# A two-block decoder on one core: streamed operands at one address residue, and the delta rule's triangular solve moved from GpSimd to VectorE

## The chip, the cores and the metric

The kernel runs on 1 core of one Trainium2 chip. The metric is the device time of one execution in microseconds, lower is better: the median of three runs before is 1069.82 us (1067.52 to 1071.11).

## What is computed

Two decoder blocks over 256 tokens of width 1024, all in float32. The first block mixes tokens by a gated delta rule (8 heads) and by forgetting attention (8 heads); the second has two SwiGLU layers around an attention mixer. The part that the change rewrites is the delta rule, a chunk at a time:

```python
a_mat = jnp.where(tri_strict, beta[..., None] * kk * decay, 0.0)
rhs = jnp.concatenate([v * beta[..., None], k * (beta * jnp.exp(G))[..., None]], axis=-1)
sol = lax.linalg.triangular_solve(a_full, rhs, left_side=True, lower=True, unit_diagonal=True)
...
def step(s, inp):
    v_new = value_c - jnp.einsum('bhcd,bhde->bhce', kcum_c, s)
    o = (jnp.einsum('bhcd,bhde->bhce', qdec_c, s) + jnp.einsum('bhcs,bhse->bhce', attn_c, v_new))
    s = s * dec_c[..., None, None] + jnp.einsum('bhcd,bhce->bhde', kdec_c, v_new)
    return s, o
```

Around it stand the weight products: `w_in` (q, k, v, z, gates of both mixers), `w_proj_gdn`, `w_proj_fox`, `w_out`, an MLP of width 4096 (relu squared), then in block 2 `gate`, `up` and `down` of width 2816 twice, and a mixer's `w_in` and `w_out`.

## The kernel before

**Weight products.** Every float32 product is made of three TensorE matmuls (hi times hi, hi times lo, lo times hi). A weight tile of 128x128 is the stationary operand, an activation tile of 128 x 256 tokens streams past it. L249 to L251 are the three matmuls of the common form, L280 to L282 a form with 512 columns, L321 to L323 the products of part of the inner dimension. SP loads raw weights, 1 MB at a time, into three buffers; ScalarE casts the high part (`wh`, L213), VectorE subtracts it for the low part (`wl`, L214), into five buffers each. The activations that stream lie in the tiles `Ah`, `Al`, `Bh`, `Bl`, `ah`, `al`, `oa2`, `ob2` (h for high, l for low), each put by `operand` with an offset of its own:

```python
    off = {"Ah": 40, "Al": 0, "Bh": 8, "Bl": 0}
```

**Order.** One generator yields the weight products in their order (the main line), others (the sides) yield the small work of norms, heads and groups with a PE time and a wait; `Lines` steps a side when its wait is over. A scheduler then sorts the instructions of each engine by a timeline of its own. What comes out is a fixed list for each engine, which runs in that order: an instruction that waits holds up all that stand behind it.

**The delta rule.** `gdn_group` handles two heads in two chunks of 128 tokens (four 128x128 matrices); there are four groups. Each makes the decay matrix by matmuls of `sel` with the rows of gate sums (L683, L684), the products K K and K Q (L696), the scaled matrix `bm` (L699), and inverts it: the diagonal blocks of 16 are cut out by DMA (`img`, then `blk`), solved by 15 steps of two GpSimd instructions (`stmp` L724, `sol` L728), put back by DMA (`inv`, then `tt`), transposed (L749), and doubled to 32, 64 and 128 by matmuls (L763, L771, L774, L780, L785). Then come the applications to V and the state (L793 to L820), the norm of the output by an inverse root on GpSimd (L139 to L147), and a transpose back (L840). Groups 0 and 1 run beside the `w_in` products, groups 2 and 3 beside `w_in`, `w_proj_fox` and the first half of `w_proj_gdn`. Forgetting attention adds its gate sums by `sel` matmuls as well (L925, L927).

After the groups the first half of the rows of `w_proj_gdn` (heads of groups 0 and 1) is multiplied, each pair of tiles being taken up by VectorE (`zt`, L1051) and GpSimd (L1054); the second half needs the output of groups 2 and 3; `w_out` follows.

Of the kernel before, what the change touches and what calls it, by code (L numbers as in the profile page):

```python
# [8 lines left out]
F32 = mybir.dt.float32  # L9
# [220 lines left out]
MM = 0.109  # L230
# [101 lines left out]
def xpair(g, slot):  # L332

    off = {"Ah": 40, "Al": 0, "Bh": 8, "Bl": 0}
    return tuple(operand(g.xp, KT, off[slot + p], slot + p, nm(g, slot + p)) for p in "hl")


def gemm_add(g, src, nk, x, scale, nxt):

    for m in range(0, KT, 2):  # L340
        if m + 2 < KT:
# [17 lines left out]
class Norm:  # L359
# [69 lines left out]
    def scales(self):  # L429

        g, nc = self.g, self.g.nc
        self.column()
        yield 1.0, 7.5
# [71 lines left out]
def gates_small(g, pool, ps, u):  # L505

    nc = g.nc
    zr = pool.tile([24, T], F32, tag="zr", name="zr")
# [67 lines left out]
    g.beta, g.ngc, g.eg, g.ed, g.rows = beta, ngc, eg, ed, rows  # L576
# [44 lines left out]
def image_views(flat):  # L621

    image = flat.rearrange("(i r) x -> i (r x)", i=4)[:, 0 : P * P].rearrange("i (s c) -> s i c", c=P)
    diag = flat[:, 0:2048].rearrange("b (j c) -> b j c", c=P)[:, :, 0:16]
    return image, diag


def gdn_group(g, grp, have, zg):

    nc = g.nc  # L630
    h0 = grp * 2
    par = grp % 2
# [18 lines left out]
    beta, ngc, eg = cols(g.beta), cols(g.ngc), cols(g.eg)  # L651
    ed = g.ed[:, h0 : h0 + 2]
    x0, x1, at, uu, tt, xp, xq, xk = (buf(n) for n in ("x0", "x1", "at", "uu", "tt", "xp", "xq", "xk"))


    ss = small([P, 8], "ss")
    pk, pq = bank(), bank()
    for a, b in ((0, pk), (1, pq)):
        for i, (h, c) in enumerate(inst):
            nc.tensor.transpose(b[:, i], kq[:, a, h, c * P : (c + 1) * P], g.ident)  # L660

    kdn, ken = xk[:, 0:2], xk[:, 2:4]
# [11 lines left out]
    nc.vector.tensor_scalar_add(sk, sk, 4 * EPS)  # L674

    nc.vector.reciprocal(bk2, sk)
    nc.vector.tensor_tensor(out=bk2, in0=bk2, in1=beta, op=ALU.mult)
    yield 0.0, 0.0

    dec = x0  # L680
    pd = raw_bank().rearrange("p (h n) -> p h n", h=2)
    for h in range(2):
        nc.tensor.matmul(pd[:, h], lhsT=g.sel[h0 + h], rhs=g.rows, start=True, stop=False)  # L683
        nc.tensor.matmul(pd[:, h], lhsT=g.identr, rhs=g.mgdnr, start=False, stop=True)  # L684
    for i, (h, c) in enumerate(inst):
        nc.scalar.activation(
            out=dec[:, i], in_=pd[:, h, c * P : (c + 1) * P], func=AF.Exp, bias=ngc[:, i : i + 1]
        )
    yield 0.45, 0.0

    bm = x1
# [13 lines left out]

    flat = g.dr.tile([32, 2064], F32, tag="img", name=nm(g, "img"), bufs=4)
    image, diag = image_views(flat)
    inv_image, inv_diag = image_views(g.inv[par])
    blk = g.gs.tile([32, 16, 16], F32, tag="blk", name=nm(g, "blk"))
    sol = g.gs.tile([32, 16, 16], F32, tag="sol", name=nm(g, "sol"))  # L710
    tmp = g.gs.tile([32, 64], F32, tag="stmp", name=nm(g, "stmp"))
    nc.sync.dma_start(out=image, in_=bm)
    yield 0.0, 0.0
    nc.sync.dma_start(out=blk, in_=diag)
# [3 lines left out]
    gp.tensor_tensor(out=nkv, in0=nkv, in1=r, op=ALU.mult)  # L718
    gp.tensor_scalar(out=base, in0=ss[:, 4:8], scalar1=P * EPS, scalar2=4 * P * EPS * EPS, op0=ALU.mult, op1=ALU.add)
    gp.tensor_copy(sol, g.con["eye16"][0:32].rearrange("p (i k) -> p i k", k=16))  # L720
    for jj in range(15):
        n, m = 15 - jj, jj + 1
        t = tmp[:, : n * m].rearrange("p (i k) -> p i k", k=m)
        gp.tensor_tensor(  # L724
            out=t, in0=blk[:, jj, m:].unsqueeze(2).to_broadcast([32, n, m]),
            in1=sol[:, jj, 0:m].unsqueeze(1).to_broadcast([32, n, m]), op=ALU.mult,
        )
        gp.tensor_tensor(out=sol[:, m:, 0:m], in0=sol[:, m:, 0:m], in1=t, op=ALU.subtract)  # L728
        if jj % 3 == 2:
            yield 0.0, 0.0  # L730
# [11 lines left out]
    nc.sync.dma_start(out=inv_diag, in_=sol)  # L742
    yield 0.0, 0.0
    for i in range(2):
        nc.sync.dma_start(out=tt[:, 2 * i : 2 * i + 2], in_=inv_image[:, 2 * i : 2 * i + 2])
    yield 0.0, 0.0
    pt = bank()
    for i in range(4):
        nc.tensor.transpose(pt[:, i], tt[:, i], g.ident)  # L749
    nc.scalar.copy(uu, pt)  # L750

    for lev, b in enumerate((16, 32)):
        def half(a, side):
            v = a.rearrange("p i (n t b) -> p i n t b", t=2, b=b)
            return v[:, :, :, side]

        p2 = (xp, xq)[lev % 2]
        nc.gpsimd.memset(half(p2, 1), 0.0)
        mask = g.con[f"m{b}"].rearrange("p (n b) -> p n b", b=b)
        nb = 64 // b  # L760
        pp = raw_bank()[:, :256].rearrange("p (i n b) -> p i n b", i=4, b=b)
        for i in range(4):
            nc.tensor.matmul(pp[:, i], lhsT=bm[:, i], rhs=half(tt, 0)[:, i], start=True, stop=True)  # L763
        nc.vector.tensor_tensor(
            out=half(p2, 0), in0=pp, in1=mask.unsqueeze(1).to_broadcast([P, 4, nb, b]), op=ALU.mult
        )
        yield 0.45, 0.0
        pu = raw_bank()[:, :256].rearrange("p (i n b) -> p i n b", i=4, b=b)
        pe = raw_bank()[:, :256].rearrange("p (i n b) -> p i n b", i=4, b=b)
        for i in range(4):  # L770
            nc.tensor.matmul(pe[:, i], lhsT=uu[:, i], rhs=half(p2, 0)[:, i], start=True, stop=True)  # L771
        nc.vector.tensor_tensor(out=half(tt, 0), in0=half(tt, 0), in1=pe, op=ALU.subtract)
        for i in range(4):
            nc.tensor.matmul(pu[:, i], lhsT=p2[:, i], rhs=half(uu, 1)[:, i], start=True, stop=True)  # L774
        nc.vector.tensor_tensor(out=half(uu, 1), in0=half(uu, 1), in1=pu, op=ALU.subtract)
        yield 0.9, 0.0
    lo, up = slice(0, 64), slice(64, P)
    pp = raw_bank()[:, :256].rearrange("p (i n) -> p i n", i=4)
    for i in range(4):
        nc.tensor.matmul(pp[up, i], lhsT=bm[lo, i, up], rhs=tt[lo, i, lo], start=True, stop=True)  # L780
    nc.vector.tensor_copy(xp[up, :, lo], pp[up])
    yield 0.45, 0.0
    pu = raw_bank()[:, :256].rearrange("p (i n) -> p i n", i=4)
    for i in range(4):
        nc.tensor.matmul(pu[lo, i], lhsT=xp[up, i, lo], rhs=uu[up, i, up], start=True, stop=True)  # L785
    nc.vector.tensor_tensor(out=uu[lo, :, up], in0=uu[lo, :, up], in1=pu[lo], op=ALU.subtract)
    yield 0.45, 0.0

    vnew = x0
# [761 lines left out]
```

## Time and profile before

| what | value |
|---|---|
| median of three runs | 1069.82 us |
| the profiled execution | 1070.23 us |
| its span, first to last instruction | 1068.4 us |
| PE busy | 1041.8 us, 98% |
| VectorE (DVE) busy | 658.7 us, 62% |
| ScalarE (ACT) busy | 566.5 us, 53% |
| GpSimd (POOL) busy | 271.4 us, 25% |
| mean granted clock of PE | 0.993 |

Engine time is time in instructions of that engine; a matmul's busy time overlaps its neighbour's, so that the pace of PE is better read from how many matmuls a stretch of the span holds than from the length of one.

### The profile page before, as it was taken

Reading aid. Unit: us, or ns where it says so; the run is one execution under the profiler, and the core shown is the slowest. Engines: PE = TensorE matmul, PEld = TensorE weight load, DVE = VectorE, ACT = ScalarE, POOL = GpSimd, SP = SyncE. Lnnn points to the kernel's source line nnn. Section 1 sums busy time; section 2 is a strip of 40 time slices with the busy share of each in tenths; the row PEclk is TensorE's granted clock in tenths of the full one; section 3 lists DMA queues with packets and bytes.
Section 4 is the critical chain, followed back from the end, with each engine's and each line's share of the span. In section 5 each row is a group of like instructions: output and inputs, shape, how many; then the busy total and the mean of one; then the engine's idle time right before and its main releaser. Section 6 shows DMA issues by size and latency. Waiting matters only on the chain.

```text
span 1068.4 us, 20471 instructions
## 1 busy us (share of the span) xinstructions
PE 1041.8 (98%) x8326; PEld 1004.9 (94%) x8326; DVE 658.7 (62%) x943; ACT 566.5 (53%) x1040; POOL 271.4 (25%) x561
## 2 busy tenths in 40 slices
PE   8999999999899899999999999999999999999997
PEld 7778899899899899999999999999989899999996
DVE  6565874757345687764555665586676576656453
ACT  6775674467345356664444444445575755444442
POOL 3635336326504240000012211141204531111000
PEclk9999999999899999999999999999999999999999
DMA  8553335334424355555454555466644445544551
GB/s 307 204 190 119 125 140 174 121 118 149 134 99 142 119 208 184 198 197 182 174 198 160 195 186 175 143 235 208 225 136 166 145 158 198 175 182 160 163 184 47
DMA packets 36271, 179.61 MB, mean 168 GB/s; under 512 B 7632, under 2 KB 11856, under 8 KB 18384
## 3 DMA queue, kind: packets, MB, share of 16 engines
q1 hardware_dynamic: 35296, 175.15, 47.2%
q0 software_dynamic: 448, 2.62, 0.7%
q8 instruction: 65, 1.06, 0.4%
q10 hardware_dynamic: 432, 0.53, 0.1%
q14 instruction: 30, 0.25, 0.1%
HBM read 175.54 MB, written 2.75 MB: 167 GB/s over the span
## 4 chain that ended last, share of the span: by engine, by line
PE 82%; POOL 9%; DMA 3%; DVE 2%; issue 2%; ACT 1%; SPq 0%; DVEq 0%; POOLq 0%; ACTq 0%
PE g L251 21%; PE g L250 21%; PE g L249 21%; PE g L282 2%; PE g L280 2%; PE g L281 2%; POOL sol L728 2%; POOL stmp L724 1%; DVE wl L214 1%; POOL rsq L144 1%; POOL rsq L145 1%; POOL rsq L146 1%; PE g L321 1%; PE g L322 1%; PE g L323 1%
## 5 line engine op out<-in xcount | busy, mean ns | idle before, releaser
L214 DVE TENSOR_TENSOR wl<-raw,wh 128x1024 fp32r<-128x1024 f32 (+2 forms) x347 | 418.6, 1211 | 263.3 <-ACT wh L213 261.3
L213 ACT CAST wh<-raw 128x1024 fp32r<-128x1024 f32 (+2 forms) x347 | 344.6, 999 | 377.1 <-PE g L250 340.1
L250 PE MATMUL g<-Bl,wh 128*128 128x256 f32 x832 | 234.0, 282 | 0.8 <-DVE Bl L169 0.8
L251 PE MATMUL g<-Bh,wl 128*128 128x256 f32 x832 | 234.0, 282 | 0.6 <-DVE wl L214 0.6
L249 PE MATMUL g<-Bh,wh 128*128 128x256 f32 x832 | 232.4, 281 | 0.0
L251 PE MATMUL g<-Ah,wl 128*128 128x256 f32 x776 | 218.2, 282 | 0.0
L250 PE MATMUL g<-Al,wh 128*128 128x256 f32 x776 | 218.2, 282 | 0.0
L249 PE MATMUL g<-Ah,wh 128*128 128x256 f32 x776 | 217.8, 282 | 0.0
L251 PE MATMUL g<-ah,wl 128*128 128x256 f32 x608 | 171.3, 282 | 1.5 <-DVE wl L214 1.5
L249 PE MATMUL g<-ah,wh 128*128 128x256 f32 x608 | 171.4, 282 | 0.0
L250 PE MATMUL g<-al,wh 128*128 128x256 f32 x608 | 171.4, 282 | 0.0
L250 PEld LDWEIGHTS g<-Bl,wh 128*128 128x128 f32 x832 | 156.7, 188 | 1.2 <-DVE Bl L169 1.2
L251 PEld LDWEIGHTS g<-Bh,wl 128*128 128x128 f32 x832 | 156.7, 188 | 0.9 <-DVE wl L214 0.8
L249 PEld LDWEIGHTS g<-Bh,wh 128*128 128x128 f32 x832 | 156.1, 188 | 0.0
L249 PEld LDWEIGHTS g<-Ah,wh 128*128 128x128 f32 x776 | 146.9, 190 | 0.5 <-ACT fv L163 0.2
L250 PEld LDWEIGHTS g<-Al,wh 128*128 128x128 f32 x776 | 146.7, 189 | 0.6
L251 PEld LDWEIGHTS g<-Ah,wl 128*128 128x128 f32 x776 | 146.8, 189 | 0.3
L251 PEld LDWEIGHTS g<-ah,wl 128*128 128x128 f32 x608 | 115.3, 190 | 1.7 <-DVE wl L214 1.7
L250 PEld LDWEIGHTS g<-al,wh 128*128 128x128 f32 x608 | 115.4, 190 | 0.0
L249 PEld LDWEIGHTS g<-ah,wh 128*128 128x128 f32 x608 | 115.2, 190 | 0.0
L1112 POOL TENSOR_TENSOR s<-s,row 128x512 f32<-128x512 f32 x22 | 36.9, 1679 | 184.2 <-ACT s L1111 184.2
L395 POOL TENSOR_TENSOR acc<-acc,sq 128x512 f32<-128x512 f32 x10 | 13.9, 1393 | 237.5 <-ACT sq L390 237.5
(332 smaller groups left out, 1444.8 us busy)
## 6 DMA issues: line engine op xcount, KB each, us to landing
raw<-in_w_in_dram SPq DMA_DIRECT2D x44, 1024.0 KB, 4.8
raw<-in_ffn_gu_dram SPq DMA_DIRECT2D x44, 1024.0 KB, 4.8
raw<-in_ffn_dn_dram SPq DMA_DIRECT2D x32, 704.0 KB, 4.1
raw<-in_w_up_dram SPq DMA_DIRECT2D x16, 1024.0 KB, 4.7
raw<-in_w_down_dram SPq DMA_DIRECT2D x16, 1024.0 KB, 4.7
raw<-in_w_out_dram SPq DMA_DIRECT2D x8, 1024.0 KB, 4.7
raw<-in_w_proj_fox_dram SPq DMA_DIRECT2D x4, 1024.0 KB, 4.9
raw<-in_w_proj_gdn_dram SPq DMA_DIRECT2D x4, 1024.0 KB, 4.8
```

Of the source, the lines that this page charges most:

```text
L144: e.tensor_tensor(out=t, in0=y, in1=y, op=ALU.mult)
L213: nc.scalar.copy(hi[:, r], raw[:, r])
L214: nc.vector.tensor_tensor(out=lo[:, r], in0=raw[:, r], in1=hi.bitcast(F32)[:, r], op=ALU.subtract)
L249: nc.tensor.matmul(out, lhsT=w_h, rhs=xh[:, k, :], start=(k == 0), stop=False)
L250: nc.tensor.matmul(out, lhsT=w_h, rhs=xl[:, k, :], start=False, stop=False)
L251: nc.tensor.matmul(out, lhsT=w_l, rhs=xh[:, k, :], start=False, stop=(k == nk - 1))
L280: nc.tensor.matmul(ps[b][t], lhsT=a_h, rhs=w_h, start=(k == 0), stop=False)
L281: nc.tensor.matmul(ps[b][t], lhsT=a_l, rhs=w_h, start=False, stop=False)
L282: nc.tensor.matmul(ps[b][t], lhsT=a_h, rhs=w_l, start=False, stop=(k == KT - 1))
L395: e.tensor_tensor(out=acc, in0=acc, in1=sq, op=ALU.add)
L728: gp.tensor_tensor(out=sol[:, m:, 0:m], in0=sol[:, m:, 0:m], in1=t, op=ALU.subtract)
L1112: nc.gpsimd.tensor_tensor(out=s, in0=s, in1=u.row2, op=ALU.mult)
```

## The change

**Addresses.** All offsets of streamed tiles become 0, and the constants shrink, with the effect that every streamed activation tile starts 64 bytes above a multiple of 256 bytes. Before, the starts above a multiple of 256 bytes were: 64 for the `A` tiles, 96 for the `B` tiles, `oa2` and `ob2`, 128 for the MLP's `ah`, 192 for `ah` of the first SwiGLU, and 0 for `ah` of the second.

```diff
-    off = {"Ah": 40, "Al": 0, "Bh": 8, "Bl": 0}
-    return tuple(operand(g.xp, KT, off[slot + p], slot + p, nm(g, slot + p)) for p in "hl")
+    return tuple(operand(g.xp, KT, PLACE.get(slot + p, 0), slot + p, nm(g, slot + p)) for p in "hl")
...
-        ah = operand(act, nf, 8, "ah", "ah")
+        ah = operand(act, nf, 0, "ah", "ah")
...
-        ah = operand(act, nf, 24 if after else 40, "ah", nm(g, "ah"))
+        ah = operand(act, nf, 0, "ah", nm(g, "ah"))
```

**Gate sums by reads.** The `sel` matmuls go; `rows_everywhere` reads the sums from DRAM to all partitions by a DMA that GpSimd issues, and GpSimd adds the mask. In the heads the sum comes in with the mask that the softmax adds anyway (`fb`).

```diff
+def rows_everywhere(g, out, r0, b0, mask, masked):
...
+    nc.gpsimd.dma_start(out=out, in_=g.rows[r0 : r0 + n, b0 * P : b0 * P + w].unsqueeze(0).to_broadcast([P, n, w]))
+    v = out.rearrange("p n (b c) -> p n b c", c=P)[:, :, masked]
+    nc.gpsimd.tensor_tensor(
+        out=v, in0=v, in1=mask.unsqueeze(1).unsqueeze(1).to_broadcast([P, n, v.shape[2], P]), op=ALU.add
+    )
```

**The solve.** Blocks of 32 of two groups stand on all 128 partitions (class `Pair`); 31 steps of two VectorE instructions solve them, in place of 15 steps of two GpSimd instructions for each group. One DMA writes the result to DRAM, one for each group reads it back, four instructions of VectorE and ScalarE spread it, and a VectorE transpose makes the other side. One doubling by matmuls is left (L839, L846 of the new kernel); the step from 64 to 128 is made while applying (`apply`, L860, L865, L870), and the state enters as K S. Waits between the steps are written as `HOP = 2.5`.

```diff
+        for jj in range(31):
+            n, m, w = 31 - jj, jj + 1, jj // 4 + 1
+            t = tmp[:, : n * w].rearrange("p (i k) -> p i k", k=w)
+            v.tensor_tensor(
+                out=t, in0=blk[:, jj, m:].unsqueeze(2).to_broadcast([P, n, w]),
+                in1=sol[:, jj, 0:w].unsqueeze(1).to_broadcast([P, n, w]), op=ALU.mult,
+            )
+            v.tensor_tensor(out=sol[:, m:, 0:w], in0=sol[:, m:, 0:w], in1=t, op=ALU.subtract)
+            if jj % 4 == 3:
+                yield 0.0, 1.5
+        nc.sync.dma_start(out=self.out.rearrange("a (n i) c -> (a n) (i c)", n=4), in_=sol.rearrange("p i c -> p (i c)"))
...
+    def apply(c):
...
+        for h in range(2):
+            nc.tensor.matmul(ps[:, h], lhsT=uu[:, 2 * h + c], rhs=vn[:, 2 * h + c], start=True, stop=True)
+        nc.vector.tensor_copy(y[lo], ps[lo, 0:2])
+        yield 0.45, HOP
...
+            nc.tensor.matmul(ps[:, h], lhsT=bm[:, 2 * h + c], rhs=y[:, h], start=True, stop=True)
+        nc.vector.tensor_tensor(out=vn[up, i], in0=vn[up, i], in1=ps[up, 0:2], op=ALU.subtract)
...
+            nc.tensor.matmul(ps[:, h], lhsT=uu[:, 2 * h + c], rhs=vn[:, 2 * h + c], start=True, stop=True)
```

**Groups.** Groups 0 and 1 start together, groups 2 and 3 share one `Pair`, and both of these wait for the two before them:

```diff
+        groups, zs = [ln.spawn(gdn_group(g, i, haves[i], zg, pair)) for i in range(2)], set()
...
-            while i >= 2 and not before[i - 2].done:
+            while not before[i - 2].done:
...
-                if i == 3:
-                    ln.finish(groups[0])
```

**Norms and w_out.** `scales`, which turns a norm's sums into row factors, makes its inverse root (14 small instructions) on VectorE in place of GpSimd, its wait goes from 7.5 to 5.5; the first two tiles of `w_out` take their last two inner steps together at the end (`gemm_first`).

```diff
-        self.column()
-        yield 1.0, 7.5
+        self.column(rsqrt=rsqrt_cols_vector)
+        yield 1.0, 5.5
...
+    for ks in (range(nk - 2), range(nk - 2, nk)):
+        for j, (hi, lo) in enumerate(units):
```

**What moves on the engines.** Before, on PE, beside the products of `w_proj_fox` (`g` tiles from `Ah`, `Bh`): the steps of groups 2 and 3 (`w` tiles; uu_2558 and tt_2559 belong to group 2, tt_3078 and x_456 to group 3) with weight products between them.

```order
1630 L251 MATMUL g_3686<-Ah_98,wl_3628 128x256
1631 L771 MATMUL w_2854<-xq_2561,uu_2558 128x64 x4
1632 L774 MATMUL w_2853<-uu_2558,xq_2561 128x64 x4
1633 L749 MATMUL w_3314<-con,tt_3078 128x128 x4
1634 L763 MATMUL w_3321<-tt_3078,x_456_3075 128x64 x4
1635 L249 MATMUL g_3686<-Ah_98,wh_3627 128x256
1636 L250 MATMUL g_3686<-Al_99,wh_3627 128x256
1637 L251 MATMUL g_3686<-Ah_98,wl_3628 128x256
1638 L249 MATMUL g_3686<-Ah_98,wh_3627 128x256
1639 L780 MATMUL w_2871<-tt_2559,x_386_2556 64x64 x4
```

In the changed kernel, on PE, where the last product of the first half of `w_proj_gdn` (`g_3778`, row 1881) ends and groups 2 (uu_3029) and 3 (uu_3050) begin their steps:

```order
1879 L349 MATMUL g_3778<-Ah_3349,wh_3679 128x256
1880 L350 MATMUL g_3778<-Al_3350,wh_3679 128x256
1881 L351 MATMUL g_3778<-Ah_3349,wl_3680 128x256
1882 L839 MATMUL w_3824<-tt_3030,x_436_3027 128x64 x4
1883 L839 MATMUL w_3830<-tt_3051,x_444_3048 128x64 x4
1884 L846 MATMUL w_3836<-uu_3029,xp_3031 128x64 x4
1885 L846 MATMUL w_3843<-uu_3050,xp_3052 128x64 x4
1886 L860 MATMUL w_3850<-vt_2102,uu_3029 128x128 x2
1887 L860 MATMUL w_3854<-vt_2428,uu_3050 128x128 x2
1888 L865 MATMUL w_3858<-xp_3031,x_436_3027 128x128 x2
1889 L865 MATMUL w_3862<-xp_3052,x_444_3048 128x128 x2
```

The steps of both groups now stand in one block, rows 1882 to 1909, without a weight product; row 1910 is the first of the second half of `w_proj_gdn`.

In the changed kernel, on VectorE, the start of the second solve (`sol_3024` and `blk_3023` are the pair of groups 2 and 3; `zt_3821` takes up the tile `g_3778` of the rows above):

```order
468 L703 TENSOR_TENSOR stmp_3416<-blk_3023,sol_3024 128x30
469 L221 TENSOR_TENSOR wl_4014<-raw_3779,wh_4013 128x1024
470 L707 TENSOR_TENSOR sol_3024<-sol_3024,stmp_3416 128x30
471 L1135 SCALAR_TENSOR_TENSOR zt_3821<-gate_1588,g_3778 128x512
472 L703 TENSOR_TENSOR stmp_3416<-blk_3023,sol_3024 128x29
473 L221 TENSOR_TENSOR wl_4049<-raw_4046,wh_4048 128x1024
474 L707 TENSOR_TENSOR sol_3024<-sol_3024,stmp_3416 128x29
475 L703 TENSOR_TENSOR stmp_3416<-blk_3023,sol_3024 128x28
```

Before, the solve of group 2 stood on GpSimd, so that no row of VectorE was part of it; now four of its 62 instructions (rows 466 to 468 and 470) stand ahead of `zt_3821` and 58 behind it, up to row 530, with one weight split (row 473) among them.

## Rows read from the trace of the kernel before

**Rows 1.** Spans and clock of the cores.
```profile
core 0: 1068.4 us, clock 0.993
```

**Rows 2.** The page, section 1: busy time, share, instructions.
```profile
PE 1041.8 (98%) x8326; PEld 1004.9 (94%) x8326; DVE 658.7 (62%) x943; ACT 566.5 (53%) x1040; POOL 271.4 (25%) x561
```

**Rows 3.** Windows of PE: stretch, length, busy (matmuls), clock, DMA share, GB/s.
```profile
163.00:183.00 20.00, 20.00 (x172) 1.00 0.53 175
276.50:282.50 6.00, 6.00 (x29) 0.50 0.46 174
...
405.00:470.00 65.00, 65.00 (x576) 1.00 0.56 195
480.00:560.00 80.00, 80.00 (x669) 1.00 0.52 183
590.00:690.00 100.00, 100.00 (x847) 1.00 0.50 173
715.00:755.00 40.00, 40.00 (x342) 1.00 0.69 236
```

**Rows 4.** Timeline of PE: start, length, line, operation, matmul records.
```profile
110.73 0.38 PE L927 MATMUL w<-rows,sel 48*128 48x256 f32 x1
111.04 0.49 PE L924 MATMUL w<-fk,fq 128*128 128x128 f32 x2
...
203.93 0.67 PE L780 MATMUL w<-tt,x 64*64 64x64 f32 x8
204.53 0.38 PE L251 MATMUL g<-Ah,wl 128*128 128x256 f32 x1
...
216.76 1.06 PE L774 MATMUL w<-uu,xq 128*128 128x64 f32 x8
217.63 0.36 PE L251 MATMUL g<-Ah,wl 128*128 128x256 f32 x1
...
217.95 0.38 PE L808 MATMUL w<-tt 128*128 128x128 f32 x2
218.17 0.39 PE L807 MATMUL w<-vt,uu 128*128 128x128 f32 x2
```

**Rows 5.** Waits of PE by line and releaser: total, times, longest.
```profile
PE w L749 <- DMA tt<-inv: 5.7, 4, 2.7
PE w L436 <- POOL col L147: 4.9, 5, 1.9
...
PE g L321 <- ACT Ah L168: 1.5, 1, 1.5
```

**Rows 6.** Timeline of VectorE, two dependent small instructions at the end.
```profile
1061.96 0.16 DVE L157 SCALAR_TENSOR_TENSOR rsq<-rsq,ms 128x2 f32<-128x2 f32 x1
1062.16 0.16 DVE L158 SCALAR_TENSOR_TENSOR col<-rsq,col 128x2 f32<-128x2 f32 x1
```

**Rows 7.** VectorE and ScalarE by line and shape: busy us, mean ns, idle before.
```profile
L214 DVE TENSOR_TENSOR wl<-raw,wh 128x1024 fp32r<-128x1024 f32 x279 | 349.1, 1255 | 216.5 <-ACT wh L213 215.2 <-PE w L1142 0.8
...
L828 ACT ACTIVATE xq<-x 128x128 f32<-128x128 f32 x16 | 4.8, 302 | 0.8 <-DVE x L824 0.7
...
L702 DVE TENSOR_TENSOR at<-w,x 128x128 f32<-128x128 f32 x16 | 4.5, 281 | 0.0
...
L842 DVE SCALAR_TENSOR_TENSOR zg<-w,gz,zg 128x512 f32<-128x512 f32 x4 | 3.0, 746 | 0.0
```

**Rows 8.** DMA issues: count, KB each, median us to landing.
```profile
tt<-inv SPq DMA_DIRECT2D x8, 128.0 KB, 2.2
...
inv<-sol SPq DMA_DIRECT2D x4, 32.0 KB, 1.7
```

**Rows 9.** Timeline of VectorE and GpSimd in one group's inverse root.
```profile
246.48 1.22 DVE L214 TENSOR_TENSOR wl<-raw,wh 128x1024 fp32r<-128x1024 f32 x1
...
246.64 1.16 POOL L142 TENSOR_SCALAR rsq<-so 128x4 f32<-128x4 f32 x1
...
248.04 0.20 POOL L145 TENSOR_TENSOR rsq<-rsq 128x4 f32<-128x4 f32 x1
248.32 0.23 POOL L146 TENSOR_SCALAR rsq<-rsq 128x4 f32<-128x4 f32 x1
```

More of the change, by code (lines that the diff above doesn't have):

```diff
@@ L260, in gemm_pair, with gemm_first @@
         yield from gemm_tile(g, ps[:, j], x, nk)
+    return ps
+def gemm_first(g, x, nk):
+    nc = g.nc
+    xh, xl = x
+    ps = [gbank(g)[:, :T] for _ in range(2)]
+    units = [g.feed.next()[0] for _ in range(2)]
+    for ks in (range(nk - 2), range(nk - 2, nk)):
+        for j, (hi, lo) in enumerate(units):
+            for k in ks:
+                w_h = hi[:, k * P : (k + 1) * P]
+                w_l = lo[:, k * P : (k + 1) * P]
+                nc.tensor.matmul(ps[j], lhsT=w_h, rhs=xh[:, k, :], start=(k == 0), stop=False)
+                nc.tensor.matmul(ps[j], lhsT=w_h, rhs=xl[:, k, :], start=False, stop=False)
+                nc.tensor.matmul(ps[j], lhsT=w_l, rhs=xh[:, k, :], start=False, stop=(k == nk - 1))
+                if k % 2 == 1:
+                    yield 6 * MM
     return ps
@@ L332, in xpair @@
 def xpair(g, slot):
-    off = {"Ah": 40, "Al": 0, "Bh": 8, "Bl": 0}
-    return tuple(operand(g.xp, KT, off[slot + p], slot + p, nm(g, slot + p)) for p in "hl")
+    return tuple(operand(g.xp, KT, PLACE.get(slot + p, 0), slot + p, nm(g, slot + p)) for p in "hl")
 def gemm_add(g, src, nk, x, scale, nxt):
     for m in range(0, KT, 2):
-        if m + 2 < KT:
+        if m == 0 and nk == KT:
+            ps = yield from gemm_first(g, src, nk)
+            for j in range(2):
+                add_tiles(g, x, ps[j].unsqueeze(1), j, 1, scale, None)
+            nxt.pair(0)
+        elif m + 2 < KT:
             ps = yield from gemm_pair(g, src, nk)
@@ L673, in gdn_group @@
     sk = ss[:, 0:4]
[L674 to L691, printed above, removed]
     for h in range(2):
@@ L703, in gdn_group @@
         yield 0.9, 0.0
[L706 to L714, printed above, removed]
+    yield from pair.load(par, bm)
     rsqrt_cols(g, r, sk, f"rsq{par}")
@@ L741, in gdn_group @@
     yield 0.45, 0.0
[L742 to L747, printed above, removed]
-    for i in range(4):
[L749 to L776, printed above, removed]
@@ L777, in gdn_group @@
-    lo, up = slice(0, 64), slice(64, P)
[L778 to L786, printed above, removed]
@@ L787, in gdn_group @@
-    yield 0.45, 0.0
-    vnew = x0
-    nkc, st = tt[:, 0:2], tt[:, 2:4]
-    ps = bank()
-    for h in range(2):
-        nc.tensor.matmul(ps[:, h], lhsT=uu[:, 2 * h], rhs=vn[:, 2 * h], start=True, stop=True)
-    for h in range(2):
-        nc.tensor.matmul(ps[:, 2 + h], lhsT=ken[:, h], rhs=uu[:, 2 * h + 1], start=True, stop=True)
-    for h in range(2):
-        scale_rows(g, vnew[:, 2 * h], ps[:, h], bk2[:, 2 * h : 2 * h + 1])
-    nc.scalar.mul(nkc, ps[:, 2:4], -1.0)
-    yield 0.9, 0.0
+    while not pair.done:
+        yield 0.0, 0.5
@@ new lines, in gdn_group @@
+    packed = xp[:, 0]
+    nc.sync.dma_start(
+        out=packed.rearrange("p (a c) -> p a c", c=8), in_=pair.out[16 * par : 16 * par + 16].rearrange("a p c -> p a c")
+    )
+    yield 0.0, 7.0
+    for n in range(4):
+        o = tt[:, :, 32 * n : 32 * n + 32].rearrange("p i (c q) -> p i c q", q=4)
+        w = packed.rearrange("p (q i c) -> p i c q", q=4, i=4)
+        col = g.con["blocks"][:, n : n + 1]
+        if n % 2:
+            nc.vector.tensor_scalar_mul(o, w, col)
+        else:
+            scale_rows(g, o, w, col)
@@ new lines, in gdn_group, with half @@
+    nc.vector.transpose(uu.rearrange("p i n -> p (i n)"), tt.rearrange("p i n -> p (i n)"))
+    def half(a, side):
+        v = a.rearrange("p i (n t b) -> p i n t b", t=2, b=32)
+        return v[:, :, :, side]
+    nc.gpsimd.memset(half(xp, 1), 0.0)
+    yield 0.0, 3.5
+    mask = g.con["m32"].rearrange("p (n b) -> p n b", b=32)
+    pp = raw_bank()[:, :256].rearrange("p (i n b) -> p i n b", i=4, b=32)
+    for i in range(4):
+        nc.tensor.matmul(pp[:, i], lhsT=bm[:, i], rhs=half(tt, 0)[:, i], start=True, stop=True)
@@ new lines, in gdn_group @@
+    nc.vector.tensor_tensor(
+        out=half(xp, 0), in0=pp, in1=mask.unsqueeze(1).to_broadcast([P, 4, 2, 32]), op=ALU.mult
+    )
+    yield 0.9, HOP
+    pu = raw_bank()[:, :256].rearrange("p (i n b) -> p i n b", i=4, b=32)
+    for i in range(4):
+        nc.tensor.matmul(pu[:, i], lhsT=xp[:, i], rhs=half(uu, 1)[:, i], start=True, stop=True)
+    nc.vector.tensor_tensor(out=half(uu, 1), in0=half(uu, 1), in1=pu, op=ALU.subtract)
+    lo, up = slice(0, 64), slice(64, P)
+    y, st = xp[:, 0:2], xp[:, 2:4]
@@ L800, in gdn_group @@
+    yield from apply(0)
     ps = bank()
@@ L993, in chain @@
                 def chain(half, pre, fq, fk, fv, hp):
-                    while not (small.done and pre[0].done and pre[1].done):
+                    while not small.done:
+                        yield 0.0, 1.0
+                    fb = g.fx.tile([P, 2, 3 * P], F32, tag="fb", name=nm(g, "fb"))
+                    rows_everywhere(g, fb, 8 + 4 * half + 2 * hp, 0, g.con["mfox"], slice(0, 3, 2))
+                    yield 0.0, 6.0
+                    while not (pre[0].done and pre[1].done):
                         yield 0.0, 2.8
-                    yield from fox_heads(g, half, hp, fq, fk, fv, ob)
+                    yield from fox_heads(g, half, hp, fq, fk, fv, fb, ob)
                 for hp in range(2):
                     heads.append(ln.spawn(chain(half, pre, fq, fk, fv, hp), 1.0 + 2.0 * hp))
-            have = {}
-            yield from gdn_project(g, u, 0, have)
+            haves = [{}, {}]
+            for i in range(2):
+                yield from gdn_project(g, u, i, haves[i])
             ln.finish(small, *heads)
```

212 lines of the change are left out of this document (123 added, 89 removed).

## The prediction

> **What bounds the kernel now.** I read four views in turn. The spans [rows 1] give 1068.4 us for the profiled execution, at a mean PE clock of 0.993; its time was 1070.2, which is 0.4 above the median of the runs. The page's busy times [rows 2] say that PE works for 1041.8 us of that, 98%: nothing but PE time and PE waits can move the end by much. VectorE at 62% and GpSimd at 25% count only where PE waits for them. The windows [rows 3] then show at what pace PE works. Each of the rows at full clock holds nothing but 256-column matmuls of one tile, and counts two that were in flight at its start; with two taken off, the A tiles go at 20/170 = 0.1176 us in one stretch and at 65/574 = 0.1132 in another, the MLP's `ah` (480 to 560) at 0.1199, the B tiles (590 to 690) at 0.1183, the first SwiGLU's `ah` (715 to 755) at 0.1176. The pace goes with the tile that streams, not with the load on the DMA queues, which read 0.50 to 0.56 in most of them. The only tiles seen at 0.1132 are those that start 64 above 256. Last, the waits of PE [rows 5]: all are small, and the largest, 5.7 us for the inverse coming back by DMA (`tt`), is the delta rule's.
>
> **The change, part by part.**
>
> **Addresses.** By the shapes, 768 matmuls stream the MLP's `ah`, 2496 a B tile (2 x 1056 in the SwiGLU ups, 192 in `w_proj_fox`, 192 in `w_out`), 192 `oa2` and `ob2`, 528 the first SwiGLU's `ah`, 528 the second's (no row here; taken as the B tiles). If all go at 0.1132 they save 768 x 0.0067 + 2688 x 0.0051 + 528 x 0.0044 + 528 x 0.0051 = 23.8 us. If all go at the slower pace of the A tiles, 0.1176, they save 768 x 0.0023 + 2688 x 0.0007 + 528 x 0.0007 = 4.1 us, and the MLP's up product, which is at 0.1132 now [rows 3], could lose 768 x 0.0044 = 3.4. What decides between the two paces of one tile no row tells; a stretch keeps the pace with which it began, for 65 us in the one row and 20 in the other. I take three quarters of the way, **-18** (bounds -1 and -24).
>
> **PE work of the groups and heads.** Prices from start to start [rows 4]: a `sel` matmul 0.31 (110.73 to 111.04), a float32 matmul of two records 0.22 (eight records 216.76 to 217.63, two 217.95 to 218.17), a 64x64 one 0.15 (eight records 203.93 to 204.53), a transpose of one record half of 0.22. Gone are 32 matmuls with `sel` or its mask (-9.9), 24 transposes (-2.6), 16 of L763 (-3.5), 48 of the 64 of L771 and L774 (-10.6), and the 32 of L780 and L785 (-4.8). The applications go from 48 to 72 matmuls (+5.3). Sum **-26** (bounds -22, if a matmul that is no longer there only lets the next one wait, and -28). It is PE time on a busy PE, so it counts in full.
>
> **The jam of groups 2 and 3.** This is the price. Before, their steps stand between weight products; now rows 1882 to 1909 stand in one block, behind the last product of the first half of `w_proj_gdn`. VectorE's 58 remaining solve instructions stand behind `zt_3821`, which reads that very product. So PE cannot have its next row before this chain is through, and nothing covers it:
> - `zt` 0.75 (as a 128x512 instruction), one split 1.26 [rows 7], and 58 solve instructions. Two small dependent ones start 0.20 apart [rows 6]; a 128x128 one takes 0.28 against 0.16 [rows 7, 6], some 1 ns for an element, and the solve's have 50 on average (3120 elements in 62), so 0.25 each: 14.5. Together 16.5.
> - the result out by DMA 1.7, in again 2.2 (the nearest transfers [rows 8]; the new ones are cut in smaller pieces, up to 5 each), the spreading and the VectorE transpose about 1.3. Sum so far **22** (bounds 18, with 0.20 for an instruction, and 28).
> - twelve steps of matmuls, taken up by VectorE at 0.28 or more each, two groups in turn, so that about half of each take-up and its hand-over lies open: **4** (2 to 8).
> - the output norm: eight squares of 0.30 on ScalarE [rows 7] 2.4, two inverse roots of 15 GpSimd instructions at 0.28 from start to start [rows 9] 8.4, scaling 1.2, take-up and split 1.5: **14** (10 to 18). Of this nothing lies beside weight products either, since row 1910 reads the outcome.
> - the clock. After a PE wait of 2.7 us [rows 5] the granted clock was 0.50, 1.2 GHz, for 6.0 us, in which 27 records went at 0.222 [rows 3], against 53 at full speed: 3 us lost. Two long waits, so **6** (3 to 12).
>
> That is 46. What goes in return are today's waits for `tt`, 5.7, and the 3 us at 1.2 GHz behind one of them: net **+37** (bounds +24 and +57). Groups 0 and 1 have weight products between all their steps, and PE's order has them late enough; I add **+2** (0 to 5) for the first pair's final transposes, behind GpSimd's new mask instructions.
>
> **Small parts.** The `scales` inverse root is 14 instructions on either engine; at 0.20 in place of 0.28 it is 1.1 us shorter, more where GpSimd is held up, but the planned wait is 2.0 shorter as well. PE waits 4.9 us for this in five places now [rows 5]: **-1** (bounds -5 and +4). `gemm_first` gives back the wait of 1.5 for the activations of `w_out` [rows 5]: **-1.5**. The DMA broadcasts, the squares from the diagonal of K K and the packed reads cost PE nothing as long as they come before their consumers, which for groups 0 and 1 the weight products hide; in the jam they are in the sum.
>
> **Sum.** 1070.2 - 18 - 26 + 37 + 2 - 1 - 1.5 = 1062.7 for a profiled execution, **1062** for the median.
>
> **A rule of the skill on the solve.** In the row of the trace, a GpSimd instruction that takes 0.20 took 1.16, inside a VectorE split of 1.22 [rows 9]; so the two engines do hold each other up, by 0.96 at a time. The Trainium skill, page "SBUF — State Buffer", section "Who interferes with whom", says that a VectorE instruction with two inputs in SBUF and a GpSimd instruction that reads SBUF exclude each other for the whole instruction, and that "issue order, not op shape, decides who blocks"; the row agrees, and by the rule the solve's instructions can be those that wait, as it has GpSimd's gate sums beside it.
>
> **The rivals.**
> - *The jam is cheap and the streams are all fast.* Lower bounds of the jam (18 + 2 + 10 + 3 = 33, less 8.7) and -24 for the addresses: 1070 - 24 - 26 + 24 - 3 = **1041**. For it: the four solve instructions ahead of `zt` and the splits could be over early. Against it: each of the 58 needs the result of the one before. Chance 0.20.
> - *Slower: VectorE's solve is held up in the jam.* Place: rows 472 to 530 of VectorE. Price: if one in four of the 58 loses the 0.96 of [rows 9], 14 us more, and the packed reads at 5 each, 6 more: jam 66, net 57. Then 1070 - 18 - 26 + 57 + 2 - 2 = **1083**. It decides from a jam of some 54 us on (18 + 26 + 8.7 + 2.5 less 2). Against it: GpSimd has only a few instructions left at that point, PE being at a stop. Chance 0.13.
> - *The addresses do nothing that counts.* If the pace belongs to something else that goes with the stage, or all streams fall into 0.1176: 1070 - 4 - 26 + 37 + 2 - 2 = **1077**. For it: the same tile shows both paces. A page speaks for this rival: the Trainium skill, "SBUF — State Buffer", "Operand start alignment", asks of an operand's start only that it be a multiple of the element size. No pace is given there, and the five paces of [rows 3] speak against it. Chance 0.17.
>
> **How the numbers follow.** The forecast, 1050 to 1074 by its own bounds, has chance 0.50; the rivals 0.20, 0.13 and 0.17. Of the forecast's 0.50, 0.13 lies within 0.3% of before (1066.6 to 1073, about what a measurement of this kernel can tell from no change), 0.02 above and 0.35 below. Faster by over 0.3%: 0.20 + 0.35 + 0.02 = 0.57; within 0.3%: 0.13 + 0.04 = 0.17; slower: 0.02 + 0.12 + 0.12 = 0.26. The range takes in the cheap jam's 1041 and the held-up solve's 1083 at their edges: 1040 to 1083.
>
> **What would show it.** In the profile after, PE's waits should have one of about 22 us before L839 and one of about 14 before L919 or row 1910, between the two halves of `w_proj_gdn`, with a granted clock of 0.50 behind each; no wait for `tt` at L749's place. The windows of the MLP's down and of both SwiGLUs should hold 8.83 matmuls to the us (0.1132) in most stretches; a count of 8.5 shows the address part wrong. PE's busy share should fall below 98%. The prediction is wrong if the wait at L839 is under 10 us (VectorE's solve was not held by `zt`) or if the streams keep their paces.

## The result, and the profile after

The changed kernel takes 1061.2 us (median of 5 runs, 1058.9 to 1062.6) against 1070.8 for the kernel before in the same job: ratio 0.9911, 95% interval 0.9887 to 0.9936, that is 9.5 us faster. The forecast was 1062. That the two agree so closely is luck: as the experiments show, two parts of the sum were wrong by about the same amount in opposite directions.

The page's busy times and the span of the profiled execution (its own time 1059.8), to set beside [rows 1, 2]:
```profile
core 0: 1058.0 us, clock 0.975
...
PE 1006.4 (95%) x8126; PEld 976.3 (92%) x8126; DVE 695.6 (66%) x1194; ACT 558.9 (53%) x1000; POOL 204.9 (19%) x379
```
PE is busy for 35 us less, but only 10 us have left the span: PE now waits, and its mean clock is lower. PE's waits, beside [rows 5], say where:
```profile
PE w L839 <- ACT tt L170: 28.6, 1, 28.6
PE w L919 <- ACT tt L170: 8.7, 2, 6.9
...
PE g L349 <- ACT Ah L175: 0.2, 1, 0.2
```
The first row is the jam of groups 2 and 3: PE cannot begin their first step, the doubling at L839, until the second pair's solve is back. The second row holds the wait for the output norm behind it. Of the waits before, those for the inverse (`tt` by DMA, 5.7) and for the `scales` columns (4.9) are gone. The one of 1.5 for `Ah` is 0.2; it stands before the second half of `w_proj_gdn`, which now has the output norm's wait ahead of it.

The windows over the stretches of [rows 3], and one in the second SwiGLU's up product:
```profile
405.00:470.00 65.00, 65.00 (x554) 1.00 0.53 186
480.00:560.00 80.00, 80.00 (x682) 1.00 0.53 187
590.00:690.00 100.00, 100.00 (x852) 1.00 0.49 174
715.00:755.00 40.00, 40.00 (x356) 1.00 0.69 236
...
890.00:990.00 100.00, 100.00 (x885) 1.00 0.53 184
```
With two taken off each count, a matmul now takes 0.1178, 0.1176, 0.1176, 0.1130 and 0.1133 us. Every streamed tile starts at 64, and there are still two paces. The MLP's up product (405 to 470), whose start did not change, lost its 0.1132; the last two stretches gained it.

The jam on PE's timeline:
```profile
292.48 0.28 PE L351 MATMUL g<-Ah,wl 128*128 128x256 f32 x1
321.34 3.67 PE L839 MATMUL w<-tt,x 128*128 128x64 f32 x16 [28.58 <-ACT tt L170]
324.81 3.62 PE L846 MATMUL w<-uu,xp 128*128 128x64 f32 x16
...
340.29 1.73 PE L899 MATMUL w<-x,at 128*128 128x128 f32 x14
348.89 2.64 PE L919 MATMUL w<-con,tt 128*128 128x128 f32 x8 [6.88 <-ACT tt L170]
```
And the granted clock over it (columns as in [rows 3]):
```profile
292.50:321.30 28.80, 0.26 (x3) 0.55 0.38 87
321.30:351.70 30.40, 23.31 (x128) 0.72 0.01 1
351.70:356.70 5.00, 4.95 (x21) 0.50 0.02 3
```
From the last product of the first half (292.5) to the clock's return (356.7), PE does little that it could not have done in a fraction of the time. The stretch costs 28.8 for the wait; 30.4 less 128 records at 0.11 [rows 4], 14.1, is 16.3; and half of the last 5.0, at 1.2 GHz, is 2.5: **47.6 us**, where the sum had 46.

VectorE at the head of that wait, the `blk` products (L703) and subtractions (L707) of the solve:
```profile
295.68 1.27 DVE L703 TENSOR_TENSOR stmp<-blk,sol 128x31 f32<-128x31 f32 x1 [2.31 <-DMA blk<-img]
296.98 0.21 DVE L707 TENSOR_TENSOR sol<-sol,stmp 128x31 f32<-128x31 f32 x1
...
298.59 0.68 DVE L1135 SCALAR_TENSOR_TENSOR zt<-gate,g 128x512 f32<-128x512 f32 x1
...
315.42 0.17 DVE L707 TENSOR_TENSOR sol<-sol,stmp 128x8 f32<-128x8 f32 x1
320.38 0.56 DVE L823 TENSOR_SCALAR tt<-xp,con 128x128 f32<-128x128 f32 x2 [4.79 <-DMA xp<-solved]
```
So 3 us of the wait stand before the solve, for the DMA of the blocks; 20 are the solve; nearly 5 the two DMAs behind it; the last 1 spreads the result. `zt` ran at 298.6, after the solve had begun.

### The profile page after: what moved, and what is told of

The parts are those of the page before. It is cut to its first block, busy times and chain, and to the rows that moved or that the text cites. A ratio compares the mean times of both kernels' runs of the same rounds, so it can differ in the third digit from the quotient of the medians.

```text
span 1058.0 us, 20140 instructions
## 1 busy us (share of the span) xinstructions
PE 1006.4 (95%) x8126; PEld 976.3 (92%) x8126; DVE 695.6 (66%) x1194; ACT 558.9 (53%) x1000; POOL 204.9 (19%) x379
## 4 chain that ended last, share of the span: by engine, by line
PE 65%; DVE 4%; POOL 2%; DMA 1%; ACT 1%; issue 1%; SPq 0%; DVEq 0%; ACTq 0%; POOLq 0%
PE g L259 19%; PE g L258 19%; PE g L260 19%; DVE wl L221 1%; PE g L349 1%; PE g L350 1%; PE g L351 1%; DVE sol L707 1%; DVE stmp L703 1%; PE g L310 1%; PE g L308 1%; PE g L309 1%; PE w L1226 1%; POOL rsq L153 0%; PE w L949 0%
## 5 line engine op out<-in xcount | busy, mean ns | idle before, releaser
L260 PE MATMUL g<-Bh,wl 128*128 128x256 f32 x816 | 227.6, 280 | 0.0
L259 PE MATMUL g<-Bl,wh 128*128 128x256 f32 x816 | 227.5, 279 | 0.0
L258 PE MATMUL g<-Bh,wh 128*128 128x256 f32 x816 | 227.0, 279 | 0.0
L259 PEld LDWEIGHTS g<-Bl,wh 128*128 128x128 f32 x816 | 153.2, 188 | 0.2
L260 PEld LDWEIGHTS g<-Bh,wl 128*128 128x128 f32 x816 | 153.2, 188 | 0.1
L427 POOL TENSOR_TENSOR acc<-acc,sq 128x512 f32<-128x512 f32 x10 | 14.1, 1413 | 244.5 <-ACT sq L422 244.5
```

The source lines that it names most:

```text
L258: nc.tensor.matmul(out, lhsT=w_h, rhs=xh[:, k, :], start=(k == 0), stop=False)
L259: nc.tensor.matmul(out, lhsT=w_h, rhs=xl[:, k, :], start=False, stop=False)
L260: nc.tensor.matmul(out, lhsT=w_l, rhs=xh[:, k, :], start=False, stop=(k == nk - 1))
L427: e.tensor_tensor(out=acc, in0=acc, in1=sq, op=ALU.add)
```

## The experiments

Differences between kernels of two jobs are taken as differences of their ratios, times 1070.8 us.

**The starts in the changed kernel.** The change with the starts of before:
```diff
-PLACE = {}
+PLACE = {"Bh": 8}
...
-        ah = operand(act, nf, 0, "ah", "ah")
+        ah = operand(act, nf, 8, "ah", "ah")
...
-        ah = operand(act, nf, 0, "ah", nm(g, "ah"))
+        ah = operand(act, nf, 24 if after else 40, "ah", nm(g, "ah"))
```


> The changed kernel with the tile starts of before (96 for B, 128, 192 and 0 for ah), all else kept. Theory (the start of the streamed tile sets the pace): the windows of the MLP's down go back to 0.1199 us a matmul, those of the B tiles to 0.1183, and the time rises by 10 to 18 us over the changed kernel's 1061, to 1071 to 1079. Rival (the start does nothing, the pace goes with the stage): paces and time stay, 1061.

Measured: 1070.4 us, ratio 0.9983 (0.9970 to 0.9996). Its windows:
```profile
405.00:470.00 65.00, 65.00 (x554) 1.00 0.53 187
480.00:560.00 80.00, 80.00 (x669) 1.00 0.52 184
590.00:690.00 100.00, 100.00 (x848) 1.00 0.51 178
```
The old paces are back, 0.1199 and 0.1182, except that the MLP's up product, whose start did not differ, stays at 0.1178. The starts are worth 0.72%, 7.7 us (by the two intervals, 3 more or less), in the changed kernel, under the 10 to 18 expected; all the rest of the change is worth 1.8. The slower pace of the MLP's up product, 768 x 0.0046 = 3.5 us by the counts, stands against that 1.8 and not in the 7.7.

**The starts alone, in the kernel before.**
```diff
-    off = {"Ah": 40, "Al": 0, "Bh": 8, "Bl": 0}
+    off = {"Ah": 40, "Al": 0, "Bh": 0, "Bl": 0}
...
-        ah = operand(act, nf, 8, "ah", "ah")
+        ah = operand(act, nf, 0, "ah", "ah")
...
-        ah = operand(act, nf, 24 if after else 40, "ah", nm(g, "ah"))
+        ah = operand(act, nf, 0, "ah", nm(g, "ah"))
```
(and `bias` with offset 0)

> The kernel before with every streamed tile 64 bytes above a multiple of 256, and nothing else changed. Theory: no stretch is left above 0.118 us a matmul, each goes at 0.1133 or 0.1178, and the time falls by 4 to 24 us, 18 by the prediction's term, to 1046 to 1066. Rival (the start does nothing): 1070, with the paces of before.

Measured: 1053.0 us (1048.5 to 1057.7), ratio 0.9826 (0.9794 to 0.9858), 18.6 us faster. Its windows:
```profile
405.00:470.00 65.00, 65.00 (x576) 1.00 0.56 195
480.00:555.00 75.00, 75.00 (x665) 1.00 0.56 193
590.00:680.00 90.00, 90.00 (x797) 1.00 0.54 185
720.00:745.00 25.00, 25.00 (x214) 1.00 0.64 217
```
Here the first three go at 0.1131 to 0.1132; the first SwiGLU's down (720 to 745) goes at 0.1179. The six runs lie in two groups, 1048.5 to 1050.6 and 1055.5 to 1057.7, and the profiled one, 1050.6, is of the faster. Of the kernels that compute everything this is the fastest: the starts by themselves beat the whole change by 8 to 9 us. Pace accounts for all of it: behind 340 us the 256-column matmuls of this trace follow each other at 0.1139 us in the mean, those of the changed kernel at 0.1161, about 12 us over some 5500 of them.

**What the jam is made of.** The second pair's solve cut to 9 of its 31 steps, and in another kernel the first pair's:
```diff
-        for jj in range(31):
+        for jj in range(self.steps):
...
-                pairs.append(Pair(g))
+                pairs.append(Pair(g, 9))
```


> The changed kernel, with steps 10 to 31 of the second pair's solve left out (44 of its 62 VectorE instructions; a part of the computation is missing). Theory (PE stands waiting for just these instructions): the wait before L839, 28.6 us, falls by 44 x 0.245 = 10.8 us, and the time by the same, to 1050. Rival (another thing, the DMA of the blocks or the take-up of the last product, ends the wait as well): less than 3 us, 1058 to 1061.

> The changed kernel, with steps 10 to 31 of the first pair's solve left out (a part of the computation is missing). The products K K of groups 2 and 3 come 34 us sooner in PE's order. Theory (it is the first pair's solve, 45 us between the splits of VectorE, that makes the second late, and the second's is spread as well): the wait before L839 falls to 8 to 16 us, time 1040 to 1050. Rival (the start of the second pair does not matter, PE's order alone does): wait over 25, 1058 to 1061.

Measured, the second pair's: 1051.0 us, ratio 0.9800 (0.9777 to 0.9822), 11.9 below the changed kernel. The first pair's: 1049.7, ratio 0.9812 (0.9780 to 0.9844), 10.6 below. One wait row of each, in that order:
```profile
PE w L839 <- ACT tt L170: 18.9, 3, 17.6
```
```profile
PE w L839 <- ACT tt L170: 17.5, 3, 13.9
```
The longest wait of each row is the second pair's, so that it falls from 28.6 to 17.6 and to 13.9. In the first kernel the 44 instructions left out give 11.0 us, 0.25 each: each VectorE step of the second solve lies on PE's path. The first solve counts too, because the second pair starts behind it: the second solve began 31.2 us sooner (264.5 against 295.7) and, with splits between its steps, ended 14.1 sooner.

**Starting the second pair sooner.** The second pair waits for the last L899 of its predecessor and not for its norm:
```diff
+    g.through.add(grp)
...
-            while not before[i - 2].done:
+            while i - 2 not in g.through:
```


> The changed kernel with groups 2 and 3 starting when groups 0 and 1 have made their last matmul, not when their output is written, and with the diagonal's junk output in another tile. In PE's order the products K K of groups 2 and 3 then come 18 us sooner. Theory (the jam is a matter of when the second pair starts): the wait before L839 falls from 28.6 to 12 to 16 us, time 1046 to 1050. Rival (beside weight products the solve is spread between the splits on VectorE, as the first pair's was, 45 us for 62 instructions, and eats the gain): 1057 to 1061.

Measured: 1056.4 us, ratio 0.9851 (0.9830 to 0.9872), 6.4 below the changed kernel; the wait:
```profile
PE w L839 <- ACT tt L170: 21.5, 3, 20.9
```
The solve began 13.2 us sooner (282.5) and ended only 3.3 sooner (312.3): in part its instructions now lie between splits of 1.2 us on VectorE. Most of a sooner start is lost in that engine's queue, as the rival had it, though the time, 1056, lies between the two forecasts.

**The solves on GpSimd,** with the sooner start:
```diff
-        v = nc.vector
+        v = nc.gpsimd
```


> The changed kernel with both solves on GpSimd instead of VectorE, and the second pair started after the first pair's last matmul as in a3. In PE's order L839 of groups 2 and 3 now stands 7.6 us ahead of the last product of the first half of w_proj_gdn. Theory (VectorE, with its splits, is the wrong queue for a chain of 62 dependent instructions): the wait before L839 is under 8 us, time 1030 to 1042. Rival (GpSimd's instructions are longer and lose 1 us beside each split): wait over 15, 1050 or more.

Measured: 1056.6 us, ratio 0.9878 (0.9845 to 0.9912), no better than on VectorE. The second pair's wait before L839 fell to 8.7 us, but the first pair got one of 10.6 there. The profiled execution, at 1059.5, is the slowest of the four. The solve by line (busy, mean ns of one, idle before):
```profile
L707 POOL TENSOR_TENSOR sol<-sol,stmp 128x60 f32<-128x60 f32 (+24 forms) x62 | 26.1, 421 | 4.9
L703 POOL TENSOR_TENSOR stmp<-blk,sol 128x60 f32<-128x60 f32 (+24 forms) x62 | 25.2, 406 | 14.8 <-DMA blk<-img 10.1
```
VectorE's splits no longer stand between the steps, but an instruction takes 0.41 us in the mean instead of 0.23 (0.28 to 0.31 in the median, and over 1 us for some), and the two solves take 29.5 and 32.5 us.

**The `scales` columns back on GpSimd,** alone and with the sooner start:
```diff
-        self.column(rsqrt=rsqrt_cols_vector)
-        yield 1.0, 5.5
+        self.column()
+        yield 1.0, 7.5
```


> The changed kernel with the norms' scales as before (inverse root on GpSimd, wait 7.5). The row factors cost PE about 3.7 us more in waits over four norms, as before. Theory (which of two paces a stream at start 64 takes is settled by how PE comes into it, so that another way of interrupting it draws anew): the MLP's and the first SwiGLU's streams, all at 0.1178 in the changed kernel, change pace in part or whole, as in b1_starts64 where they ran at 0.1133; if all do, 11 us less, net 1053. Rival (the pace is fixed by the tile's place in this layout): paces stay, the waits add up, 1064 to 1065.

> a6 with the second pair started early as in a3. Theory: the 5 us of a3 come off a6 whatever its paces are: 1048 if the streams turn fast, 1059 if not.

Measured: 1067.1 us (1061.7 to 1070.6), ratio 0.9968 (0.9946 to 0.9991), 6.1 above the changed kernel; with the sooner start 1061.5, ratio 0.9926 (0.9900 to 0.9952). PE's wait for the columns is back, and three of the windows of the first kernel have other paces than the changed kernel (0.1132, 0.1133, 0.1178; these are the MLP's up and down and the second SwiGLU's up):
```profile
PE w L468 <- POOL col L154: 4.2, 5, 1.8
```
```profile
415.00:480.00 65.00, 65.00 (x576) 1.00 0.56 193
490.00:570.00 80.00, 80.00 (x708) 1.00 0.55 192
...
890.00:990.00 100.00, 100.00 (x851) 1.00 0.51 179
```
No start was touched here, and yet paces changed, in both directions: what comes earlier on PE is enough to draw them anew. The profiled execution, at 1070.4, is near the top of this kernel's runs, so its rows are not those of the median, and the 6.1 us are not fully accounted for.

**All of the change but the delta rule,** on the kernel before (the starts, the heads' sums by reads, the columns on VectorE, `gemm_first`):

> The kernel before with its own delta rule kept (blocks of 16 on GpSimd, doubling, sel matmuls in the groups), and with the other parts of the change: starts at 64, gate sums of the attention heads by reads, scales on VectorE, gemm_first. Theory (the rewritten delta rule gives back in one long wait what it saves in matmuls): this is the faster kernel, 1053 of the starts alone less some 7.6 for the heads (the two sel matmuls of a head and the slower matmuls between them) and some 5 for the norms and w_out: 1038 to 1044. Rival (the delta rule's part is a gain of its own that the tile paces only hid): not below the changed kernel less 9, 1052 or more.

Measured: 1064.4 us, ratio 0.9950 (0.9928 to 0.9971). The expectation failed. Its largest wait:
```profile
PE w L796 <- DMA tt<-inv: 10.1, 5, 6.2
```
PE now waits 10.1 us for the old delta rule's inverse, where it was 5.7, and most streams went at 0.1177; against the trace of the starts alone the slower pace is some 15 us by the counts, the larger part of the miss. The profiled execution, at 1069.4, is the slowest of the twelve. The waits led to the next two.

**Is the kernel before bound by PE's work there?** The heads' sums left out altogether (no `sel` matmul in `fox_heads`):
```diff
-        nc.tensor.matmul(sc[:, 0:P], lhsT=g.sel[8 + h], rhs=g.rows[:, 0:P], start=False, stop=True)
...
-        nc.tensor.matmul(sc[:, P:384], lhsT=g.sel[8 + h], rhs=g.rows, start=False, stop=True)
```


> The kernel before with the sel matmuls of the attention heads left out (the gate sums are missing from the scores). By the prediction's price, 16 matmuls at 0.25 to 0.31, 4.5 to 5 us less: 1065. Theory now: the other matmuls of a head get faster as well, since they no longer alternate with matmuls of the other number format, 0.95 a head, 7.6 in all: 1062 to 1063.

Measured: 1071.2 us, ratio 1.0007 (0.9985 to 1.0028): nothing. Two of its waits:
```profile
PE w L749 <- DMA tt<-inv: 7.7, 3, 4.5
PE w L840 <- ACT x L163: 3.4, 1, 3.4
```
5.4 us more than in [rows 5], one of them (L840) new. The mean granted clock fell as well:
```profile
core 0: 1069.2 us, clock 0.989
```
That is 0.4% under [rows 1], some 4 us. Together this is about what the matmuls had taken, 8 us by the heads' rows further down. Then the same with the inverse's solve cut from 15 steps to 5:
```diff
-    for jj in range(15):
+    for jj in range(5):
```


> b3 (the kernel before without the heads' sel matmuls) with steps 6 to 15 of each group's solve on GpSimd left out as well. Theory (in the kernel before it is the chain of the delta rule that sets the end of this stage, so that PE work taken away only turns into waits, as b3's 7 us did): with the chain shorter the waits for tt, 7.7 us in b3, and L840, 3.4, go, and the 7 us of PE work count at last: 1070 less 10 to 16, 1054 to 1060. Rival (the heads' matmuls were no PE time worth having): within 3 us of b3.

Measured: 1050.9 us, ratio 0.9822 (0.9791 to 0.9853), 19.8 below the same kernel with the full solve, more than expected. The largest of its waits and the delta rule's, and the clock:
```profile
PE w L436 <- POOL col L147: 4.8, 5, 1.9
...
PE w L749 <- DMA tt<-inv: 0.6, 2, 0.4
```
```profile
core 0: 1048.2 us, clock 0.998
```
Of the delta rule's two waits, 11.1 us, 0.6 are left, and the clock is back, which is 0.9% of the span, about 9 us; the two make up the 19.8. So in the kernel without these matmuls it is the chain of the delta rule, not PE's work, that sets the end of this stage. The short solve was not run with the `sel` matmuls kept: how much it gives there is not shown.

**A shorter chain without the jam?** The kernel with the starts alone, and every second group's solve on VectorE:
```diff
+    sv = nc.vector if par else gp
...
-        gp.tensor_tensor(out=sol[:, m:, 0:m], in0=sol[:, m:, 0:m], in1=t, op=ALU.subtract)
+        sv.tensor_tensor(out=sol[:, m:, 0:m], in0=sol[:, m:, 0:m], in1=t, op=ALU.subtract)
```


> b1_starts64 (the kernel before with all starts at 64), with the solves of groups 1 and 3 on VectorE and those of groups 0 and 2 on GpSimd, blocks of 16 as before. Theory (the two solves of a pair follow one another on GpSimd, and this chain sets the end of the stage; b4 says that the stage has 19 us to give): the second group of each pair is ready some 20 us sooner, the waits for tt, 5.9 us in b1, fall under 3, and the time falls by 4 to 10 us below b1, to 1043 to 1049. Rival (the chain from the first pair to the second counts, and its first group is not sooner): within 3 us of b1, 1050 to 1056.

Measured: 1056.4 us (1049.1 to 1063.5), ratio 0.9868 (0.9821 to 0.9914), no better than without it.
```profile
PE w L841 <- ACT x L163: 7.6, 2, 5.6
...
PE w L750 <- DMA tt<-inv: 2.0, 1, 2.0
```
The wait for the inverse fell to 2.0, from 5.9 with the starts alone, and a new one at the output transposes took its place. The paces differ too: the second SwiGLU's up went at 0.1178 here and at 0.1133 there (851 and 885 matmuls from 890 to 990), 4.8 us over its 1056, so that the total by itself does not tell what the shorter chain was worth.

## Why the prediction was right, and where it was not

**Addresses: mis-sized.** "I take three quarters of the way, -18": in the changed kernel the term measured -7.7, and less if the MLP's up product, which the prediction had in this term, is counted in it. A saving of that size was there to be had, since the same starts give -18.6 in the kernel before. What failed is the choice between the two paces. The prediction saw that one tile has two (0.1132 and 0.1176) and that no row tells which; of the five stretches three drew the slower one, so that the third rival came in half. The page of the Trainium skill that was to speak for that rival, "SBUF — State Buffer", section "Operand start alignment", asks of a start only that it be a multiple of the element size. That is a rule of what is legal, not of speed; between starts it allows lay 18.6 us here.

**PE work: the step that failed.** "It is PE time on a busy PE, so it counts in full." It does not: 16 `sel` matmuls taken out of the heads of the kernel before changed the time by nothing, and came back as waits of 5.4 us and a lower clock. With the solve's chain cut, 19.8 us went. So in that stage the end was held by a chain through the inverse, its solve and its DMAs, whose waits on PE were only 5.7 us in [rows 5] because PE had other rows to fill the time. A share of 98% hid this. For the delta rule's own matmuls, which left together with their chain, no run shows what they were worth.

**The heads: under-priced.** Between weight products, two heads took this in the kernel before:
```profile
109.53 0.38 PE L924 MATMUL w<-fk,fq 128*128 128x128 f32 x2
109.85 0.32 PE L925 MATMUL w<-rows,sel 48*128 48x128 f32 x1
110.10 0.70 PE L926 MATMUL w<-fk,fq 128*128 128x256 f32 x2
...
112.65 0.39 PE L250 MATMUL g<-Al,wh 128*128 128x256 f32 x1
```
and this after:
```profile
110.11 0.39 PE L1002 MATMUL w<-fk,fq 128*128 128x128 f32 x2
110.33 0.60 PE L1003 MATMUL w<-fk,fq 128*128 128x256 f32 x2
...
111.23 0.47 PE L259 MATMUL g<-Al,wh 128*128 128x256 f32 x1
```
3.12 against 1.12, so 1.0 us a head, where the sum had twice 0.31. The sum left out that the `fk,fq` matmuls between the `sel` ones are quicker without them: from start to start 0.22 in place of 0.32, and 0.44 in place of 0.63 (the next rows start at 110.73 [rows 4], and after at 110.77). For eight heads that is 3 us of PE time more.

**The jam: right in size, with parts that were not.** 47.6 against 46. Its parts: the wait at L839 28.6 against 22, just above its upper bound of 28, the norm 6.9 against 14, and steps and clock 12.1 against 10. Of these the clock is most: at half speed for the 11.6 us behind the first wait and for 7.9 us behind the norm's, it cost 9.8, where the sum had 6. What the solve waited for was wrong: not for the last product by way of `zt`, since it had begun before `zt` ran, but for its blocks, which came in by DMA at 295.7. That its serial VectorE steps set the wait was right (the short second solve).

**The rest.** The `scales` columns and `gemm_first` were -2.5. The columns' waits of 4.9 are gone. The 1.5 that `gemm_first` was to give back was not `w_out`'s: in the kernel before it stands in `w_proj_gdn`, ten us ahead of `w_out`, and where `gemm_first` is added to that kernel (all of the change but the delta rule) it is still there, as the second line shows:
```profile
350.49 0.95 PE L321 MATMUL g<-Ah,wh 128*128 128x256 f32 x4 [1.48 <-ACT Ah L168]
```
```profile
PE g L347 <- ACT Ah L175: 1.5, 1, 1.5
```
From `w_out`'s first product (360.7 and 364.2) to the end of the span the change with the old starts is 707.7 - 702.9 = 4.8 us shorter. Ahead of `w_out` that kernel is 3.5 us longer than before, where the sum without the starts had -26 + 37 + 2, 13: it lost 9.5 less than I had. Of this the heads are 3, if PE time counts there, and the jam, 44 in that kernel by the same count (its wait is 26.4), is 2; 4 to 5 were not taken apart.

**Together:** addresses 10.3 worse than forecast, all else 12.3 better (-1.8 against +10.5). So the right total is luck, and not a sign that the parts were right. The rivals: neither the cheap jam nor the held-up solve came. Of the second solve's 62 instructions two took 1.27 us in place of 0.21, each beside a GpSimd `gate` addition (L1138), 2.1 us in all. By the Trainium skill, "SBUF — State Buffer", "Who interferes with whom", a VectorE instruction with two inputs in SBUF and a GpSimd instruction that reads SBUF exclude each other for the whole instruction; the trace agrees for these two, and from 301.6 to the solve's end GpSimd has nothing to do, as argued.

## What to carry to other kernels

Before work is taken off the busiest engine, ask what chain runs beside it, and shorten that chain in a test kernel: if the time falls with the engine's work left as it is, that work was not what set the time, whatever the busy share. A chain of small dependent instructions that is moved to where no other work is left costs its full length and the clock behind it. Take a change apart before it is kept: here one of its parts alone was worth twice the whole, in part by paces that the whole did not draw.

## What was not expected of the hardware

- One streamed tile at one start runs at 0.1132 or 0.1178 us per 256-column matmul. Where they were read, a stream at this start keeps its pace until it is interrupted, even when it passes from one tile to the next: through the MLP's up and down and into the first SwiGLU the changed kernel went at 0.1177, and the kernel with the starts alone at 0.1132:
```profile
404.00:574.00 170.00, 170.00 (x1446) 1.00 0.53 188
```
```profile
401.00:567.00 166.00, 166.00 (x1468) 1.00 0.56 193
```
  Kernels that differ only in what comes earlier draw differently. The other starts have one pace each in these traces (0.1183 for the B tiles, 0.1199 for the MLP's `ah`). What decides at the beginning of a stream stays open. The runs of the kernel with the starts alone spread over 9.2 us, and those with the short second solve over 3.0, which would fit a draw in each execution; with one profile of each that was not tested.
- After the wait of 28.6 us PE worked at half its clock for 11.6 us, without a pause (321.3 to 332.9, granted clock 0.50), then at full clock, and at half again from 346.6 to 356.8, in and after the norm's wait. The 16 records of L846 that took 3.62 us there took this in the first pair, at full clock:
```profile
225.30 1.97 PE L846 MATMUL w<-uu,xp 128*128 128x64 f32 x16
```
